# Keys of a gated recurrence: TensorE transposes replaced by VectorE block transposes and a trip through DRAM

## The chip, the core and the metric

One Trainium2 chip, one of its cores. A core has TensorE (PE in the profile; its weight loads, which overlap the matmuls, are PEld), VectorE (DVE), ScalarE (ACT), GpSimd (POOL) and SyncE (SP), each with its own instruction stream in order; they wait for each other by semaphores. SP issues nearly all DMA transfers of this kernel; sixteen DMA engines carry them out. The metric is the device time of one execution in microseconds (us); lower is better.

## The reference

An encoder block over 1024 tokens of width 1024: one large projection, dilated window attention, a bidirectional gated linear recurrence (HGRN2), a gated merge, and a feed-forward layer. Only the recurrence is touched. Per head (8 heads, keys and values of width 128) and per direction it computes, in chunks:

```python
    cum = jnp.cumsum(logf.reshape(b, h, n, c, kd), axis=3)
    q_dec = q * jnp.exp(cum)
    k_inv = k * jnp.exp(-cum)
    ...
    u = jnp.einsum('bhnck,bhncv->bhnkv', k * jnp.exp(cum_last - cum), v)
    ...
    def step(state, inp):
        d, uu = inp
        return d[..., None] * state + uu, state
```

The sum `u` over the tokens of a chunk is a matrix product, keys transposed times values. TensorE contracts over the partition dimension, so it needs the keys with tokens on the partitions. The kernel holds them the other way round, with the 128 key features on the partitions and tokens along the row, since the decays are scans along the tokens.

## The kernel before

Everything is float32; large products are made as three products of split parts (hi x hi, lo x hi, hi x lo: lines 277 to 279). Phase 1 is the projection. `stream` (line 677) runs it as a sequence of 322 steps: tiles of output columns in a seven-product scheme (a Strassen-like one, order 1, 2, 6, 5, 7, 3, 4), each step 4 x 3 = 12 products of 128x512 into a PSUM bank named pj. After a step its bank is evacuated (`leave`, line 650) by ScalarE into `wkeep` or by VectorE into a buffer `evh`, of which there are three, and then stored to DRAM by SP (lines 578, 592, 605, 620). The weight blocks a11, a21, a12 and a22 of the next tile are loaded by SP (line 256) when their single buffers come free; VectorE forms sums of them (lines 717, 718, 722), ScalarE and GpSimd split them (lines 219 and 229).

Beside the stream run side jobs on the projections that are finished: per pair of heads two recurrence jobs (`hgrn_side`, line 1294), then the attention of a head group (`att_far`, `att_near`). A side job is a generator: `yield k` means that it goes on after k more steps of the stream (a negative number also lets the next job's first loads be issued). So the code's order sets a priority; a scheduler then lines up each engine's instructions, taking later ones where an earlier one's operands are not there yet. On the chip each engine keeps the order that came out.

`hgrn_side` does for a head: load its projections; for both directions (d = 0 and 1) gate activations on ScalarE, decay scans (line 1181) and reciprocals (line 1199) on VectorE, products on GpSimd (lines 1189 and 1202) that end as the scaled keys `st["ki", d]`, the tile `t0` or `t1`, 128 features x 1024 tokens. `hgrn_keys` (line 1210) turns them: for each half of the tokens b, four PE transposes of 128x128 against the identity into a PSUM bank `sd`, and one ScalarE copy to a buffer `hkT` (line 1217). `hgrn_states` (line 1221) multiplies `hkT` with the values `hv` (line 1232; four matmuls for the first half, three for the second), and folds the chunk states with ScalarE and VectorE (lines 1234 to 1243, tiles hS and hR). Then come the scores (lines 1257 to 1261), the outputs (line 1284) and the norm.

The buffers `hkT`, `ham`, `hsq`, `hon`, `bias` and `perm` share five slots of 128x512 (`half`, line 783). The value rows already take a similar way: `rows` (line 582) transposes 32x32 blocks on VectorE (line 589) and stores them with four DMAs that place the blocks (line 592).

When the last side job is done, the attention results are loaded and split (lines 1333 to 1336) during the last steps of the stream, so that phase 2 can begin with them.

Of the kernel before, what the change touches and what calls it, by code (L numbers as in the profile page):

```python
# [10 lines left out]
F32 = mybir.dt.float32  # L11
# [11 lines left out]
HALF = 512  # L23
# [56 lines left out]
class Block:  # L80
    evac_ahead = 1000

    def __init__(self, ctx, tc, x, ln_in_g, ln_in_b, w_in, hgrn_lb, hgrn_norm_g, w_att_up, w_hgrn_up,
                 w_o, ln1_g, ln1_b, w_ffn_in, w_ffn_out, ln2_g, ln2_b, tabs, out, dbg=None):
        self.tc, self.nc, self.ctx = tc, tc.nc, ctx
        self.x = x[0]
        self.ln = {"in": (ln_in_g, ln_in_b), "1": (ln1_g[0], ln1_b[0]), "2": (ln2_g[0], ln2_b[0])}
        self.w_in, self.lbw, self.ng = w_in[0], hgrn_lb, hgrn_norm_g[0]
        self.wa, self.wr, self.wo = w_att_up[0], w_hgrn_up[0], w_o[0]
        self.wfi, self.wfo, self.tabs, self.out = w_ffn_in[0], w_ffn_out[0], tabs, out[0]  # L90
        self.dbg = dbg or {}
        nc = self.nc

        self.npj = 0
        self.issued = {}
        self.psum = ctx.enter_context(tc.tile_pool(name="psum", bufs=1, space=PSUM))
        self.cst = ctx.enter_context(tc.tile_pool(name="cst", bufs=1))
        self.tiny = ctx.enter_context(tc.tile_pool(name="tiny", bufs=1))
        self.spare = self.pad(self.cst, CST_PAD)
        self.wpool = self.pool("wp", "right")  # L100
        self.wp = self.wpool.__enter__()
        dram = ctx.enter_context(tc.tile_pool(name="dram", bufs=1, space=DRAM))

        def scratch(name, n):
            if name in self.dbg:
                return [self.dbg[name][i] for i in range(n)]
            return [dram.tile([128, 1024], F32, name=f"{name}{i}") for i in range(n)]

        self.att_d = scratch("att", 4)
        self.rec_d = scratch("rec", 8)  # L110
        self.tg_d = scratch("tg", 16)
        self.n1_d = scratch("n1", 8)
        self.ahs_d = scratch("ahs", 8)
        self.hg_d = [{n: dram.tile([128, T], F32, name=f"hg{h}{n}") for n in ("t0", "t1", "q", "g")}
                     for h in range(8)]
        self.at_d = [{(k, g): dram.tile([128, T], F32, name=f"at{j}{k}{g}") for k in "qk" for g in range(3)}
                     for j in range(4)]
        for h in range(8):
            self.hg_d[h]["v"] = dram.tile([T, 128], F32, name=f"hg{h}v")
        for j in range(4):  # L120
            self.at_d[j].update({("v", g): dram.tile([T, 128], F32, name=f"at{j}v{g}") for g in range(3)})
        self.w_d = [dram.tile([32, 128], F32, name=f"wd{j}") for j in range(4)]
        self.td = [dram.tile([128, 4, HALF], F32, name=f"td{i}") for i in range(3)]
        self.gd = {p: dram.tile([128, NF // 2, HALF], F32, name=f"gd{p}") for p in range(1, 8)}
        self.consts()
# [1081 lines left out]
        nc.vector.scalar_tensor_tensor(qd[:, :, near], q3[:, :, near], CQ, qd[:, :, near], op0=OP.mult, op1=OP.mult)  # L1207
        yield

    def hgrn_keys(self, st, d):  # L1210

        nc, out = self.nc, []
        for b in (0, 1) if d == 0 else (1, 0):
            pt, kT = self.ps_sd(), self.half3("hkT")
            for k in range(4):
                nc.tensor.transpose(pt[:, 128 * k:128 * (k + 1)], st["ki", d][:, 4 * b + k, :], self.ident)
            nc.scalar.copy(kT, pt.rearrange("p (k c) -> p k c", k=4))
            out.append(kT)
        return out

    def hgrn_states(self, st, d, kT, vT):
# [72 lines left out]
    def hgrn_side(self, h, st):  # L1294
        nc = self.nc
        vT = self.fetch_rows(5, "hv", self.hg_d[h]["v"])
        st["fa"] = self.slot(6, "fa")
        steps = [self.hgrn_dir(h, d, st) for d in range(2)]
        for _ in range(2):
            for z in steps:  # L1300
                next(z)
                yield 1
        k0 = self.hgrn_keys(st, 0)
        for z in steps:
            next(z)
        yield 2
        next(steps[0])
        yield 1
        S = {0: self.hgrn_states(st, 0, k0, vT)}
        k1 = self.hgrn_keys(st, 1)  # L1310
        yield 2
        next(steps[1])
        sg = self.fetch(8, "hg", self.hg_d[h]["g"])
        yield 1
        S[1] = self.hgrn_states(st, 1, k1, vT)
        yield 3
        am = [self.hgrn_scores(st, b) for b in range(2)]
        yield -3
        on = [self.hgrn_out(st, b, am[b], vT, S) for b in range(2)]
        yield 2  # L1320
        for b in range(2):
            pt = self.ps_sd()
            for jj in range(4):
                nc.tensor.transpose(pt[:, 128 * jj:128 * jj + 128], on[b][:, jj, :], self.ident)
            s = slice(HALF * b, HALF * (b + 1))
            nc.vector.scalar_tensor_tensor(sg[:, s], pt, self.ngc, sg[:, s], op0=OP.mult, op1=OP.mult)
        nc.scalar.dma_start(self.rec_d[h], sg)
# [733 lines left out]
```

## Time and profile before

| what | value |
|---|---|
| median of 3 runs | 2019.93 us (2014.48 to 2020.14) |
| the profiled execution's own time | 2021.5 us |
| its span, first to last instruction | 2019.7 us |
| mean granted TensorE clock | 0.997 |
| line 1216, key transposes on PE | 128, from 127.9 to 932.8 us |
| line 1217, their copies by ScalarE | 32, median 592 ns |
| line 1232, state matmuls on PE | 224, from 134.7 to 941.0 us |
| DMA, mean rate | 149 GB/s |

The page gives each engine's busy time and share of the span, then 40 slices with the busy tenths. Views by window give the same per stretch, with the number of instructions in brackets, the granted clock and the DMA engines' share. A row of a timeline has start, duration, engine, line, operation and the tiles it writes and reads. A row of the waits names who waited for whom: total, times, longest. The rows of a line's view give min/median/max; an SPq row is a DMA's issue on SP's queue. Matmuls are pipelined, so the sum of durations on PE is more than the time that they take up.

### The profile page before, as it was taken

Reading aid. Unit: us, or ns where it says so; the run is one execution under the profiler, and the core shown is the slowest. Engines: PE = TensorE matmul, PEld = TensorE weight load, DVE = VectorE, ACT = ScalarE, POOL = GpSimd, SP = SyncE. Lnnn points to the kernel's source line nnn. Section 1 sums busy time; section 2 is a strip of 40 time slices with the busy share of each in tenths; the row PEclk is TensorE's granted clock in tenths of the full one; section 3 lists DMA queues with packets and bytes.
Section 4 is the critical chain, followed back from the end, with each engine's and each line's share of the span. In section 5 each row is a group of like instructions: output and inputs, shape, how many; then the busy total and the mean of one; then the engine's idle time right before and its main releaser. Section 6 shows DMA issues by size and latency. Waiting matters only on the chain. (4 is left out here: it accounts for less than half of the span.)

```text
span 2019.7 us, 30761 instructions
## 1 busy us (share of the span) xinstructions
PE 1985.0 (98%) x10782; PEld 1644.0 (81%) x10782; DVE 1338.9 (66%) x2105; ACT 932.7 (46%) x1926; POOL 1008.1 (50%) x874
## 2 busy tenths in 40 slices
PE   7999999999999999999999999999999999999998
PEld 5688888788888888788888888887788888888886
DVE  7876645885468944778454236557776776767788
ACT  6654455554555536555464332345333333344541
POOL 5566644576446663566546562244665665620000
PEclk9999999999999999999999999999999999999999
DMA  5444545455454453445537377434434443447533
GB/s 161 138 129 140 168 113 146 127 145 170 118 149 137 135 164 104 150 136 143 152 106 210 120 254 244 149 122 145 138 131 136 138 140 129 138 166 280 167 101 124
DMA packets 369404, 301.16 MB, mean 149 GB/s; under 512 B 98721, under 2 KB 308578, under 8 KB 369250
## 3 DMA queue, kind: packets, MB, share of 16 engines
q1 hardware_dynamic: 362752, 277.94, 45.7%
q10 hardware_dynamic: 6498, 21.27, 2.8%
q8 instruction: 85, 1.39, 0.3%
q14 instruction: 69, 0.57, 0.1%
HBM read 204.96 MB, written 94.18 MB: 148 GB/s over the span
## 5 line engine op out<-in xcount | busy, mean ns | idle before, releaser
L229 POOL TENSOR_TENSOR w_lo<-wa,w_hi 128x512 fp32r<-128x512 f32 x272 | 363.4, 1345 | 268.9 <-ACT w_hi L219 255.3
L219 ACT CAST w_hi<-wa 128x512 fp32r<-128x512 f32 x272 | 168.2, 620 | 242.9 <-PE pj L278 147.3
L229 POOL TENSOR_TENSOR w_lo<-wsum,w_hi 128x512 fp32r<-128x512 f32 x88 | 127.5, 1460 | 111.9 <-PE sd L279 60.7
L229 POOL TENSOR_TENSOR w_lo<-f_raw,w_hi 128x512 fp32r<-128x512 f32 x66 | 101.1, 1540 | 51.6 <-ACT w_hi L219 50.4
L215 POOL TENSOR_TENSOR mv<-mv,mhalf 128x1 f32<-128x1 f32 x16 | 12.6, 790 | 221.7 <-DVE mv L214 221.6
L219 ACT CAST w_hi<-wsum 128x512 fp32r<-128x512 f32 x88 | 54.6, 621 | 116.7 <-PE sd L278 107.0
L277 PE MATMUL pj<-xt1hi,w_hi 128*128 128x512 f32 x252 | 100.0, 397 | 0.7 <-DVE evh L589 0.7
L219 ACT CAST gwsum<-a_raw 128x512 fp32r<-128x512 f32 (+1 forms) x78 | 48.2, 618 | 112.4 <-PE pj L278 50.1
L278 PE MATMUL pj<-xt1lo,w_hi 128*128 128x512 f32 x252 | 98.5, 391 | 0.0
L279 PE MATMUL pj<-xt1hi,w_lo 128*128 128x512 f32 x252 | 98.2, 391 | 0.0
L719 POOL TENSOR_TENSOR wa<-wa,wa 128x512 f32<-128x512 f32 x46 | 66.2, 1440 | 57.9 <-DVE wa L718 51.6
L603 DVE TENSOR_TENSOR evh<-wkeep,pj 128x512 f32<-128x512 f32 x45 | 30.8, 685 | 89.0 <-PE pj L279 52.6
L229 POOL TENSOR_TENSOR w_lo<-ws,w_hi 128x512 fp32r<-128x512 f32 x46 | 61.8, 1348 | 55.3 <-ACT w_hi L219 50.7
L747 ACT COPY wkeep<-pj 128x512 f32<-128x512 f32 x136 | 79.6, 585 | 0.2 <-DVE evh L577 0.2
L277 PE MATMUL pj<-xt2hi,w_hi 128*128 128x512 f32 x192 | 76.6, 400 | 2.0 <-ACT w_hi L219 2.0
L279 PE MATMUL pj<-xt2hi,w_lo 128*128 128x512 f32 x192 | 76.3, 397 | 2.2 <-POOL w_lo L229 2.2
L229 DVE TENSOR_TENSOR gwkeep<-a_raw,gwsum 128x512 fp32r<-128x512 f32 (+1 forms) x78 | 53.2, 682 | 37.4 <-ACT gwsum L219 34.7
L277 PE MATMUL pj<-xb11hi,w_hi 128*128 128x512 f32 x192 | 75.9, 398 | 1.5 <-DVE evh L619 1.5
L278 PE MATMUL pj<-xt2lo,w_hi 128*128 128x512 f32 x192 | 76.1, 396 | 0.7 <-DVE xt2lo L409 0.6
L277 PE MATMUL pj<-xt4hi,w_hi 128*128 128x512 f32 x192 | 75.9, 395 | 0.0
L279 PE MATMUL pj<-xb11hi,w_lo 128*128 128x512 f32 x192 | 75.4, 393 | 0.0
L278 PE MATMUL pj<-xb11lo,w_hi 128*128 128x512 f32 x192 | 75.4, 393 | 0.0
(441 smaller groups left out, 6506.0 us busy)
## 6 DMA issues: line engine op xcount, KB each, us to landing
wa<-in_w_in_dram SPq DMA_DIRECT2D x184, 256.0 KB, 3.4
f_raw<-in_w_ffn_in_dram SPq DMA_DIRECT2D x44, 512.0 KB, 4.2
a_raw<-gd SPq DMA_DIRECT2D x30, 512.0 KB, 3.7
gd<-fc SPq DMA_DIRECT2D x44, 256.0 KB, 2.0
gd<-fs SPq DMA_DIRECT2D x33, 256.0 KB, 2.1
tg<-evh SPq DMA_DIRECT2D x32, 256.0 KB, 3.3
tg<-tg SPq DMA_DIRECT2D x16, 512.0 KB, 5.6
y<-ahs SPq DMA_DIRECT2D x16, 512.0 KB, 7.8
```

The costliest lines, as they stand in the source:

```text
L215: nc.gpsimd.tensor_tensor(mv[:, 2:3], mv[:, 2:3], self.mhalf[:, 0:1], OP.pow)
L219: ins = nc.scalar.copy(hi, src) if eng_hi == "act" else nc.vector.tensor_copy(hi, src)
L229: ins = e.tensor_sub(lo, src, hi.bitcast(F32))
L277: nc.tensor.matmul(ps, whi, xhi, start=first, stop=False, **kw)
L278: nc.tensor.matmul(ps, whi, xlo, start=False, stop=False, **kw)
L279: self.product = nc.tensor.matmul(ps, wlo, xhi, start=False, stop=last, **kw).ins.name
L603: self.left(nc.vector.tensor_add(t, add, ps))
L719: nc.gpsimd.tensor_sub(a["a21"], a["a22"], a["a11"])
L747: nc.scalar.copy(t, ps)
```

## The change

The key transposes and their copies go. In their place VectorE transposes each half (128x512) in 32x32 blocks in one instruction, SP stores the result to a DRAM scratch tile `kd`, and four loads per half, one for each group of 32 partitions, bring it back into the same buffer with the blocks in their places; each piece that is moved back is 32 floats, 128 bytes. Store and loads are now two functions: both directions are turned and stored early, and the loads (`hgrn_back`) are issued later in the code. One `yield 1` becomes `yield 2`.

```diff
+        self.kd = [[dram.tile([128, HALF], F32, name=f"kd{h}{n}") for n in range(4)] for h in range(8)]
...
-    def hgrn_keys(self, st, d):
+    def hgrn_keys(self, h, st, d):
 
         nc, out = self.nc, []
         for b in (0, 1) if d == 0 else (1, 0):
-            pt, kT = self.ps_sd(), self.half3("hkT")
-            for k in range(4):
-                nc.tensor.transpose(pt[:, 128 * k:128 * (k + 1)], st["ki", d][:, 4 * b + k, :], self.ident)
-            nc.scalar.copy(kT, pt.rearrange("p (k c) -> p k c", k=4))
-            out.append(kT)
+            t, scr = self.half("hkT"), self.kd[h][2 * d + b]
+            nc.vector.transpose(t, st["ki", d][:, 4 * b:4 * b + 4, :].rearrange("p k c -> p (k c)"))
+            nc.sync.dma_start(scr, t)
+            out.append((t, scr.rearrange("(a i) (k b j) -> b i k a j", a=4, b=4, j=32)))
+        return out
+
+    def hgrn_back(self, keys):
+        out = []
+        for t, z in keys:
+            for b in range(4):
+                self.nc.sync.dma_start(t[32 * b:32 * b + 32, :].rearrange("i (k a j) -> i k a j", a=4, j=32), z[b])
+            out.append(t.rearrange("p (k c) -> p k c", k=4))
         return out
...
-        k0 = self.hgrn_keys(st, 0)
+        k0 = self.hgrn_keys(h, st, 0)
         for z in steps:
             next(z)
+        k1 = self.hgrn_keys(h, st, 1)
         yield 2
+        k0 = self.hgrn_back(k0)
         next(steps[0])
-        yield 1
+        yield 2
         S = {0: self.hgrn_states(st, 0, k0, vT)}
-        k1 = self.hgrn_keys(st, 1)
+        k1 = self.hgrn_back(k1)
         yield 2
```

What the scheduler makes of it is shown at three places of the third head (the first one behind an attention job). Rows are instructions in their engine's order; xN counts equal ones in a row. The new file's line numbers are shifted: 277 to 279 become 278 to 280, 1232 becomes 1240.

PE before, at the first state group of the third head (`t_3694` is its keys of the second direction):

```order
L277 MATMUL pj<-xt2hi,w_hi 128x512
L278 MATMUL pj<-xt2lo,w_hi 128x512
L1232 MATMUL sd<-hv,hkT 128x128 x7
L1216 MATMUL sd<-tabs_sb,t_3694 128x128 x8
L279 MATMUL pj<-xt2hi,w_lo 128x512
```

PE in the change, at the first state group of the same head:

```order
L279 MATMUL pj<-xb22lo,w_hi 128x512
L1240 MATMUL sd<-hv,hkT 128x128 x4
L280 MATMUL pj<-xb22hi,w_lo 128x512
L278 MATMUL pj<-xb22hi,w_hi 128x512
L279 MATMUL pj<-xb22lo,w_hi 128x512
L280 MATMUL pj<-xb22hi,w_lo 128x512
L278 MATMUL pj<-xt4hi,w_hi 128x512
L279 MATMUL pj<-xt4lo,w_hi 128x512
L1240 MATMUL sd<-hv,hkT 128x128 x3
```

The transposes are gone, the seven state matmuls stand in two pieces, and the first piece has moved back: it stood behind the 1232nd product of the stream (the first transposes behind the 1212th), and now stands behind the 1316th; the second direction's two pieces stand behind the 1344th and the 1353rd (before: in one piece behind the 1260th).

SP before, at the same place, begins with the load of the output gate and goes on with weight loads (`wa`), stores of evacuated banks (`at1q`, `at1v`) and loads for the next steps:

```order
L801 DMA hg<-hg2g 128x1024
L256 DMA wa_4026<-in_w_in_dram 128x4x128
L801 DMA q<-hg3q 128x1024
L256 DMA wa_4052<-in_w_in_dram 128x4x128
L256 DMA wa_4108<-in_w_in_dram 128x4x128
L256 DMA wa_4128<-in_w_in_dram 128x4x128
L578 DMA at1q_154<-evh 128x512
L256 DMA wa_4149<-in_w_in_dram 128x4x128
L592 DMA at1v_183<-evh 32x16x32 x4
```

SP in the change, from the head's first key store on:

```order
L1217 DMA kd_187<-hkT 128x512
L1217 DMA kd_188<-hkT 128x512
L257 DMA wa_4099<-in_w_in_dram 128x4x128
L1217 DMA kd_190<-hkT 128x512
L1225 DMA hkT<-kd_187 32x16x32
L1217 DMA kd_189<-hkT 128x512
L1225 DMA hkT<-kd_187 32x16x32 x3
L1225 DMA hkT<-kd_188 32x16x32
L579 DMA at1q_154<-evh 128x512
L1225 DMA hkT<-kd_188 32x16x32 x3
L1225 DMA hkT<-kd_190 32x16x32 x2
L593 DMA at1v_215<-evh 32x16x32 x4
```

Twenty transfers of the keys now stand among the stores of evacuated banks; the weight loads that stood here (the a22 blocks last) come behind the last key load.

VectorE in the change, in the same head, from the evacuation of the bank that ends with the 1212th product (line 618, before 617) to both pairs of key transposes:

```order
L618 TENSOR_TENSOR pj<-wkeep,pj 128x512
L1205 SCALAR_TENSOR_TENSOR qd<-q,fa 128x8x64
L578 TENSOR_TENSOR evh<-wkeep,pj 128x512
L723 TENSOR_TENSOR wa_3616<-wa_3616,wa_3410 128x512
L723 TENSOR_TENSOR wa_3660<-wa_3660,wa_3431 128x512
L1200 RECIPROCAL qd<-fb 128x4x64 x2
L620 SCALAR_TENSOR_TENSOR evh<-evh,pj 128x512
L1200 RECIPROCAL qd<-fb 128x4x64
L1216 STREAM_TRANSPOSE hkT<-t_3769 128x512 x2
L1205 SCALAR_TENSOR_TENSOR qd<-q,fa 128x8x64
L1216 STREAM_TRANSPOSE hkT<-t_3773 128x512 x2
```

The four transposes are inserted into VectorE's row of evacuations, weight sums and reciprocals; before, that row had none for the keys.

## The prediction

> **What bounds the kernel now.** I read the page first: its head, engine line and slices.
>
> ```profile
> span 2019.7 us, 30761 instructions
> PE 1985.0 (98%) x10782; PEld 1644.0 (81%) x10782; DVE 1338.9 (66%) x2105; ACT 932.7 (46%) x1926; POOL 1008.1 (50%) x874
> PE   7999999999999999999999999999999999999998
> ```
>
> TensorE (PE) is busy in every slice and no other engine is above 66%. An average hides stages, so I cut out the stretch in which the eight recurrence heads run, where all edits lie:
>
> ```profile
> core 0: us, PE busy (x) PEld busy (x) DVE busy (x) ACT busy (x) POOL busy (x), PEclk, DMA share, GB/s
> 100.00:200.00 100.00, 99.53 (x558) 83.77 (x557) 70.92 (x81) 49.35 (x100) 65.24 (x62) 1.00 0.46 136
> 200.00:400.00 200.00, 197.13 (x1326) 164.00 (x1326) 126.74 (x261) 105.00 (x265) 104.88 (x97) 1.00 0.49 139
> 400.00:600.00 200.00, 199.40 (x1321) 166.80 (x1317) 121.96 (x253) 100.49 (x244) 111.85 (x106) 1.00 0.52 146
> 600.00:800.00 200.00, 199.01 (x1311) 166.53 (x1310) 135.93 (x241) 104.62 (x246) 119.79 (x116) 1.00 0.48 138
> 800.00:940.00 140.00, 137.48 (x800) 115.16 (x800) 109.72 (x144) 73.26 (x165) 84.08 (x79) 0.99 0.45 129
> ```
>
> PE stands idle for only 7.5 of these 840 us, at a granted clock of 0.99 to 1.00. So PE's work here is the time: what leaves PE is won in full, and each microsecond for which PE stands before an operand is lost in full. What PE waited for between 100 and 1000 us is a short list, complete here:
>
> ```profile
> PE pj L279 <- POOL w_lo L229: 2.5, 2, 2.0
> PE pj L277 <- DVE evh L619: 1.5, 1, 1.5
> PE pj L277 <- DVE evh L589: 1.2, 1, 1.2
> PE sd L1069 <- DVE WW L1066: 1.1, 2, 0.6
> PE sd L1216 <- POOL t L1202: 1.0, 1, 1.0
> ```
>
> No transfer stands in it: as the kernel is, PE never waits for DMA here.
>
> **Part 1: the transposes leave PE.** 128 of them go: eight heads, two directions, eight each. Their busy time overlaps that of their neighbours, so I price them by start times (start, duration, then the group) in the timeline:
>
> ```profile
> 127.70 0.39 PE L277 MATMUL pj<-xt2hi,w_hi 128*128 128x512 f32 x1
> 127.93 1.03 PE L1216 MATMUL sd<-tabs_sb,t 128*128 128x128 f32 x8
> 128.72 0.48 PE L278 MATMUL pj<-xt2lo,w_hi 128*128 128x512 f32 x1
> 134.71 1.72 PE L1232 MATMUL sd<-hv,hkT 128*128 128x128 f32 x14
> 136.27 1.04 PE L1216 MATMUL sd<-tabs_sb,t 128*128 128x128 f32 x8
> 137.06 0.48 PE L277 MATMUL pj<-xt1hi,w_hi 128*128 128x512 f32 x1
> ```
>
> Eight transposes hold the stream from 127.93 to 128.72, and again from 136.27 to 137.06: 0.79 us, or 0.099 us each. 128 x 0.099 = **12.7 us off PE**. (A stream product takes 127.93 - 127.70 = 0.23 us.) The switches between product and small-matmul stretches cost a little too, but I count 25 such stretches of transposes and state matmuls before and 26 after, because the state groups now stand in pieces, so that term is nil.
>
> A rule speaks against this part's aim. The Trainium skill, "VectorE: DVE Perf Modes", section "Rules for kernel authors", says to transpose 128x128 on TensorE if a PSUM destination will do. The same page, under "The three transpose paths", gives 390 ns there (bf16); by that figure the gain would be an estimated 50 us. The start times above speak against that figure inside a dense stream, and for the rule: a PE transpose is cheap here, so there is little to win.
>
> Also gone is PE's wait for GpSimd before the transposes. Whole trace, view of line 1216:
>
> ```profile
>   POOL t L1202: 2.9, 3
> ```
>
> Three of sixteen groups met it: **2.9 us**. Together 15.6 us is the most that can be won. ScalarE loses its 32 evacuations of PSUM; it is at 46% and PE does not wait for it, so nothing is booked.
>
> **Part 2: VectorE.** 32 transposes of 128x512 are added. The same operation and shape is there already, for the value rows:
>
> ```profile
> L589 DVE STREAM_TRANSPOSE evh<-evh x30: 648/700/715, 80.1 to 958.8; 128x512 f32<-128x512 f32 x30
> ```
>
> 32 x 0.70 = 22.4 us, 2.8 us a head, on an engine that is at 61 to 78% in the windows above. On average that hides in its idle time. What is queued behind: the evacuations of the stream's banks. If VectorE is just then behind, PE pays up to these 2.8 us a head, 22 us in all; I book nothing, since the list of PE's waits holds only 2.7 us for evacuations.
>
> **Part 3: the trip through DRAM.** Each head adds 4 stores of 256 KB and 16 loads of 64 KB, all on SP's queue. The nearest rows (issue min/median/max in ns, then landing in us) are the row stores with the same 128-byte pieces in the other direction, the plain stores of 256 KB, and the 64 KB gathers from DRAM in pieces of 512 bytes:
>
> ```profile
> L592 SPq DMA_DIRECT2D hg1v<-evh x8: 319/494/507, 129.4 to 154.6; - x8
> DMA to landing us min/median/max: 1.8/2.1/6.7
> L578 SPq DMA_DIRECT2D at0k<-evh x6: 320/452/902, 148.3 to 257.3; - x6
> DMA to landing us min/median/max: 2.0/2.3/4.9
> L819 SPq DMA_DIRECT2D v<-at0v x8: 430/432/1202, 262.0 to 266.3; - x8
> DMA to landing us min/median/max: 2.9/3.8/6.6
> ```
>
> From the start of a transpose to the moment when the first state group may run: transpose 0.7, store landed 2.3, three more loads issued 3 x 0.49 = 1.5, last load landed 3.5 (between 2.9 and 3.8): **8.0 us**. A load of this very shape is not in the trace; by the row stores' 2.1 the trip is 6.6 us, by the gathers' worst 6.6 it is 11.1.
>
> Does PE arrive earlier than that? Third head, the example of the order rows. PE reached its 1212th stream product, the place of the old transposes, long before VectorE evacuated the bank finished there:
>
> ```profile
> 372.29 1.09 PE L1216 MATMUL sd<-tabs_sb,t 128*128 128x128 f32 x8
> 380.48 0.68 DVE L617 TENSOR_TENSOR pj<-wkeep,pj 128x512 f32<-128x512 f32 x1
> L1199 DVE RECIPROCAL qd<-fb x32: 1687/1740/1752, 125.5 to 941.0; 128x256 f32<-128x256 f32 x32
> ```
>
> VectorE was 8.2 us behind. In the new order three reciprocals (3 x 1.74 = 5.2) and six passes over 128x512 (6 x 0.7 = 4.2 at the pace of L589) stand from that evacuation to the key transposes: they begin about 17.6 us after product 1212, and the keys are there at 25.6. The new state group stands behind stream product 1316, which PE reaches after 104 x 0.227 = 23.6 us. PE would stand there for 2.0 us. If VectorE were not behind, nothing would be waited for. The later groups add little: from the fourth load to the sixteenth SP issues 19 transfers (12 loads and 4 row stores at 0.49, 3 plain stores at 0.45: 9.2 us), and PE has 37 products and 11 of the small matmuls, 37 x 0.227 + 11 x 0.1 = 9.5 us, of other work between.
>
> So per direction the unknown lies between 0 and 2.0 us. There are 16 directions, so **0 to 32 us** in all. I take 0.44 us each, **7 us**: half of the directions meeting the 0.9 us by which the gathers' median landing exceeds their least. It is nearer to the low end because the three waits of L1216 average 0.18 us over its sixteen groups: state groups, like those, were put where their operands come. The nearest row of a similar kind is that one, but the trip is longer and has more that can vary.
>
> **Part 4: SP and DMA time.** SP gets 16 x 0.49 + 4 x 0.45 = 9.6 us of issues per head. What is queued behind a load that waits for its store is, in the order rows, an evacuation's store, whose buffer is wanted again, and weight loads. The engines' load is read from a stretch with 128-byte row stores and one of wide transfers (columns as above):
>
> ```profile
> 130.50:131.00 0.50, 0.50 (x4) 0.42 (x3) 0.50 (x2) 0.15 (x1) 0.50 (x1) 1.00 0.81 119
> 132.50:133.00 0.50, 0.50 (x4) 0.42 (x3) 0.50 (x2) 0.50 (x2) 0.28 (x1) 1.00 0.99 336
> ```
>
> A 64 KB piece at 119 GB/s and a share of 0.81 takes about 0.45 us of all sixteen engines: 16 pieces are 7.2 us a head, against windows at a share of about 0.5. I book nothing; uncovered, it is 7.2 us x 8 = 57 us. The Trainium skill, "DMA: Bandwidth & Descriptors", Specifications, puts the least size for line rate at 512 bytes; by that rule a jam is likelier than by the average share, and the two rows above agree with its direction.
>
> **Part 5: one more step per head.** The side work ends 8 steps of 12 products later: 8 x 12 x 0.227 = 22 us. What follows it must still be ready for phase 2:
>
> ```profile
> L229 POOL TENSOR_TENSOR att_lo<-st_raw,att_hi x4: 2394/2398/2407, 1096.1 to 1106.9; 128x1024 fp32r<-128x1024 f32 x4
> L277 PE MATMUL pj<-att_hi,w_hi x64: 389/389/389, 1153.4 to 1196.2; 128*128 128x512 f32 x64
> ```
>
> The last split ends at 1106.9 + 2.4 = 1109.3 and is wanted at 1153.4: 44 us of room, 22 us after the shift. Hidden; without that cover, up to 22 us.
>
> **The sum**, against the profiled execution's own 2021.5 us: -12.7 - 2.9 + 7 = -8.6, so 2012.9. That execution lay 1.6 us above the median of 2019.93; on the scale of the median it is 2011.3, rounded to **2012**.
>
> **The rivals.**
> - *Full gain.* The state groups stand late enough everywhere and PE never waits: 2019.9 - 15.6 = 2004. For it: PE's old list has no DMA in it, and only 3 of 16 transposes waited. Against it: the sum for the third head.
> - *It cancels out*: the change does not do what it says, the freed PE time comes back as waits of 0.6 to 1.35 us per direction, 10 to 22 us: 2014 to 2026, middle 2020. For it: a trip of two landings replaces a PSUM copy.
> - *Slower: PE stands before the keys in every direction*, because VectorE's backlog starts the trip late. Place: the first state matmuls of each direction; price: 2.0 us as in the third head, 16 x 2.0 = 32; 2019.9 - 15.6 + 32 = 2036. It decides from 15.6 / 16 = 0.98 us per direction. For it: the 8.2 us of backlog in a row. Against it: a wait at the first direction leaves the second more room.
> - *Slower: the weight loads behind the keys come late.* The last weight blocks of a tile (a22) now stand behind the key loads on SP. If four of the 7.2 us of a burst reach PE in each head: 8 x 4 = 32, again 2036. For it: SP is in order. Against it: the view of the weight loads shows hardly any wait on them.
>
> ```profile
>   DVE ws L717: 4.2, 4
> ```
>
> 4.2 us in four waits in the whole run: most loads come in good time. By the 512-byte rule of the Trainium skill ("DMA: Bandwidth & Descriptors", Specifications) this would be the rival to come true.
>
> **How the numbers follow.** Chances: forecast (waits of 3 to 10 us, 2007 to 2014) 0.34; full gain 0.12; cancels 0.28; slower by late keys 0.18; slower by late weights 0.08. About 0.3%, 6 us, is what a measurement of this kernel can tell from no change. Faster is 0.34 + 0.12 = 0.46, the same 0.28, slower 0.26. The range from 2003 to 2034 takes in the full gain and most of the slower cases, and leaves out some 0.15 above and little below.
>
> **What would show it.** Right: L1216 gone from PE, its stream spaced by 0.23 us there, PE idle in 100 to 940 us grown from 7.5 to 10 to 18 us, with DMA hkT<-kd among PE's releasers. The trip: key loads landing 2.9 to 3.8 us after issue. Wrong: PE's waits for hkT above 16 us (late keys), or waits for evh, w_hi and w_lo grown by more than that (VectorE or weights), or key loads landing at 6 us and more at a DMA share near 1.

## The result and the profile after

| | before | after |
|---|---|---|
| median | 2018.59 us (2014.48 to 2020.14, 4 runs) | 2036.05 us (2035.74 to 2040.20, 4 runs) |
| ratio after / before, 95% interval | | 1.0094 [1.0074, 1.0115] |
| profiled execution, its own time | 2021.5 us | 2035.74 us |
| its span | 2019.7 us | 2033.9 us |
| mean granted TensorE clock | 0.997 | 0.993 |

The change makes the kernel slower by 0.9%; the forecast was a gain of 0.4%. The transposes did leave TensorE, and that is worth what was forecast; the trip through DRAM costs two and a half times that gain. One execution of e1 (3310.8 us) and one of e4 (2478.9 us) ran at a granted clock of 0.56 and 0.75; the medians and ratios of the experiments leave these two out.

The head of the page after, and its engine line:

```profile
span 2033.9 us, 30808 instructions
PE 1980.4 (97%) x10654; PEld 1634.6 (80%) x10654; DVE 1345.2 (66%) x2137; ACT 920.9 (45%) x1894; POOL 1008.0 (50%) x874
```

PE is busy for 4.6 us less than before (1985.0) in a span that is 14.2 us longer: the loss is not more work, it is waiting and clock. Where it arises is read from the first product of phase 2 (view of the tile `att_hi`; the first of the two start times):

```profile
L278 PE MATMUL pj<-att_hi,w_hi x64: 389/389/389, 1166.2 to 1209.1; 128*128 128x512 f32 x64
```

Before it began at 1153.4 us, now at 1166.2: 12.8 of the 14.2 us are lost ahead of it, in phase 1. The windows of the stretch with the recurrence heads, which before added up to 7.5 us of idle PE at a clock of 0.99 to 1.00:

```profile
core 0: us, PE busy (x) PEld busy (x) DVE busy (x) ACT busy (x) POOL busy (x), PEclk, DMA share, GB/s
100.00:200.00 100.00, 100.00 (x548) 84.09 (x547) 76.10 (x89) 47.13 (x95) 66.96 (x63) 1.00 0.61 164
200.00:400.00 200.00, 192.76 (x1226) 158.71 (x1225) 125.84 (x253) 95.53 (x234) 106.65 (x95) 0.99 0.54 147
400.00:600.00 200.00, 195.03 (x1287) 162.12 (x1286) 124.29 (x257) 104.70 (x262) 108.28 (x102) 0.99 0.55 150
600.00:800.00 200.00, 192.55 (x1168) 159.70 (x1167) 135.24 (x225) 96.09 (x220) 117.94 (x115) 0.98 0.60 164
800.00:940.00 140.00, 137.32 (x895) 114.17 (x894) 91.44 (x159) 70.72 (x159) 72.49 (x73) 0.98 0.54 151
```

840 - 817.7 = 22.3 us are idle now, and the clock has fallen to 0.98 in the later windows. The first window, with one head in it, has no idle time at all. PE's waits between 100 and 1000 us, complete, as before:

```profile
PE sd L1240 <- DMA hkT<-kd: 6.3, 7, 2.1
PE pj L278 <- DVE evh L578: 5.0, 2, 3.9
PE sd L1268 <- ACT hS L1242: 3.7, 3, 1.9
PE pj L278 <- DVE evh L620: 3.1, 2, 1.7
PE sd L1265 <- ACT hS L1242: 1.9, 1, 1.9
PE pj L278 <- ACT wkeep L748: 1.8, 2, 1.0
PE pj L280 <- POOL w_lo L230: 1.7, 2, 1.4
PE sd L1240 <- issue: 0.9, 1, 0.9
PE sd L1240 <- PE pj L280: 0.3, 1, 0.3
```

They sum to 24.7 us, against 7.3 before. Only a quarter of them name the keys. And behind some of them, or within them, the clock is halved. The windows below are the stretches between 100 and 1000 us for which the trace records it, the clock is the third number from the end:

```profile
381.90:385.30 3.40, 3.40 (x9) 2.67 (x9) 3.40 (x4) 0.04 (x1) 3.03 (x3) 0.50 0.74 228
416.10:419.50 3.40, 3.40 (x26) 2.90 (x23) 3.40 (x6) 1.11 (x3) 1.75 (x2) 0.50 0.72 160
668.60:675.40 6.80, 5.44 (x33) 4.56 (x34) 5.42 (x11) 4.38 (x13) 3.11 (x3) 0.50 1.02 345
880.30:887.10 6.80, 6.17 (x15) 4.81 (x16) 6.80 (x7) 0.92 (x2) 5.42 (x6) 0.50 0.35 97
```

The first lies behind a wait of 3.88 us for L578, which ends at 381.40; the second behind one of 1.92 us for hS (415.48); the third among two for hS, 1.91 and 1.65 us (667.44 and 669.96); the fourth begins in a wait of 1.71 us for L620 (880.93), behind one of 0.96 us for `wkeep` (878.52).

20.4 us at half speed lose 10.2 us at the most; in the profiled execution before there was one such stretch of 3.4 us (856.4 to 859.8), 1.7 us lost. The balance of the heads: -12.7 (transposes) + 24.7 - 7.3 (waits) + 10.2 - 1.7 (clock) = +13.2, measured 12.8. (Both executions have one more stretch at half speed ahead of the heads, 6.8 us before and 3.4 us now; with it the balance is +11.5.) So the time is accounted for to within about 1 us; what is left to explain is the waits that do not name the keys.

The third head shows where two of them come from. SP's timeline, from the first key load on:

```profile
391.74 0.62 SPq L1225 DMA_DIRECT2D hkT<-kd  x1
...
396.45 3.31 SPq L1225 DMA_DIRECT2D hkT<-kd  x5
399.86 2.20 SPq L593 DMA_DIRECT2D at1v<-evh  x4
402.10 2.60 SPq L1225 DMA_DIRECT2D hkT<-kd  x4
...
406.73 0.56 SPq L1225 DMA_DIRECT2D hkT<-kd  x1
407.39 0.61 SPq L257 DMA_DIRECT2D wa<-in_w_in_dram  x1
```

SP issues almost without a pause for 15.6 us (391.74 to 407.39), and the weight block `wa` comes last. ScalarE, meanwhile, and then PE:

```profile
411.19 0.62 ACT L220 CAST w_hi<-wa 128x512 fp32r<-128x512 f32 x1 [5.43 <-DMA wa<-in_w_in_dram]
411.72 1.14 ACT L1242 ACTIVATE hS<-sd,dec 128x128 f32<-128x128 f32 x4
...
414.56 0.87 ACT L1242 ACTIVATE hS<-sd,dec 128x128 f32<-128x128 f32 x3
```

```profile
415.48 0.27 PE L1268 MATMUL sd<-qd,t 128*64 128x64 f32 x1 [1.92 <-ACT hS L1242]
```

ScalarE stands for 5.43 us before the cast of a block whose load was issued too late: at 407.39, and 3.8 us later the cast begins. The states' copies (L1242), which need nothing of that block, stand behind the cast; PE waits 1.92 us for the bank that they empty; at 416.1 the clock is halved. This is a chain, SP to ScalarE to PE, that the list of PE's waits shows only by its last link. At 665.7 us it is there again, with 4.53 us. The transfers themselves are hardly slower. The weight loads between 100 and 1000 us, from issue to landing:

```profile
L257 SPq DMA_DIRECT2D wa<-in_w_in_dram x144: 367/384/1163, 102.1 to 998.1; - x144
DMA to landing us min/median/max: 2.8/3.6/8.9
```

Before the change the median was 3.4 us, and in e2 below, which has no trip, 3.5 us with a worst case of 8.5. In the burst (391.7 to 407.4) the DMA engines' share is 0.71, so they are not full there; from 661 to 665.7, at the second place, it is 0.89.

### The profile page after: what moved, and what is told of

Same layout as the page of the kernel before. It is cut to its first block, busy times and chain, and to the rows that moved or that the text cites. A ratio compares the mean times of both kernels' runs of the same rounds, so it can differ in the third digit from the quotient of the medians.

```text
span 2033.9 us, 30808 instructions
## 1 busy us (share of the span) xinstructions
PE 1980.4 (97%) x10654; PEld 1634.6 (80%) x10654; DVE 1345.2 (66%) x2137; ACT 920.9 (45%) x1894; POOL 1008.0 (50%) x874
## 5 line engine op out<-in xcount | busy, mean ns | idle before, releaser
L279 PE MATMUL pj<-xt4lo,w_hi 128*128 128x512 f32 x192 | 75.9, 395 | 0.0
```

The source lines that it names most:

```text
L279: nc.tensor.matmul(ps, whi, xlo, start=False, stop=False, **kw)
```

## The experiments

Two theories stand against each other. **Late keys**: what costs is that PE stands before the loads of the keys. **The queue**: what costs is that twenty transfers a head on SP put off what stands behind them. Beside them VectorE's transposes and the extra step could be the cause. Each experiment was timed in three rounds beside the kernel before; "us" is the median. e2, e5, e11, e12 and e15 do not compute the reference's result: their state products read other numbers.

| kernel | us | ratio to before, 95% interval |
|---|---|---|
| e2: no trip | 2004.11 | 0.9935 [0.9920, 0.9950] |
| e11: stores only | 2009.51 | 0.9963 [0.9947, 0.9979] |
| e15: stores, tiny loads, late states | 2011.66 | 0.9974 [0.9957, 0.9990] |
| e5: trip, unread | 2019.36 | 1.0004 [0.9993, 1.0014] |
| e12: trip unread, late states | 2029.02 | 1.0059 [1.0042, 1.0077] |
| **the change** | 2036.05 | 1.0094 [1.0074, 1.0115] |
| e16: weight loads ahead of keys | 2037.41 | 1.0100 [1.0084, 1.0115] |
| e9: stores place the blocks | 2041.36 | 1.0124 [1.0102, 1.0146] |
| e6: without the extra step | 2043.46 | 1.0128 [1.0110, 1.0147] |
| e1: key loads on ScalarE's queue | 2045.34 | 1.0138 [1.0119, 1.0156] |
| e7: half the trip | 2029.70 | 1.0056 [1.0039, 1.0073] |
| e4: before, with the extra step | 2023.63 | 1.0028 [1.0014, 1.0041] |
| e3: before, with 32 VectorE transposes | 2021.96 | 1.0016 [1.0006, 1.0026] |

### The parts that are not the trip: e3, e4, e2

e3 is the kernel before with the transposes added:

```diff
+            nc.vector.transpose(self.half("hkD"), st["ki", d][:, 4 * b:4 * b + 4, :].rearrange("p k c -> p (k c)"))
```

> The kernel before, keys turned by TensorE as ever, plus the 32 VectorE transposes of 128x512 into a buffer that nobody reads. VectorE theory: 8 to 22 us over before, 2027 to 2041, with PE's waits for DVE evh up from 2.7 us. Queue and step theory: within 4 us of before.

It is 0.16% slower, some 3 us. VectorE's 22 us of work are hidden but for that.

e4 is the kernel before with `yield 2` for `yield 1` ahead of the states of direction 0:

> The kernel before with the one yield 1 turned into yield 2, so each recurrence job takes one more step of the stream; nothing else. Step theory: 2025 to 2036, PE waits of 10 us and more for DVE evh. Queue and VectorE theory: 2014 to 2023, same as before.

It is 0.28% slower, some 6 us. In its profiled execution the longest of PE's waits is

```profile
PE pj L277 <- DVE evh L577: 4.3, 2, 3.8
```

The changed kernel has the same wait (L578 above, 3.9 us at the longest), before its third head's key loads. There is no trip in e4, so the step is enough for it. It is not the step alone that sets its length: e2, e5 and e11 below have the step too, but their state products earlier, and show 1.9 us there.

e2 is the changed kernel without stores and loads:

```diff
-            nc.sync.dma_start(scr, t)
...
-            for b in range(4):
-                self.nc.sync.dma_start(t[32 * b:32 * b + 32, :].rearrange("i (k a j) -> i k a j", a=4, j=32), z[b])
...
-                nc.tensor.matmul(ps[:, jj, :], kT[b][:, c % 4, :], vT[:, c, :], start=True, stop=True)
+                nc.tensor.matmul(ps[:, jj, :], vT[:, c, :], vT[:, c, :], start=True, stop=True)
```

> Store and loads are left out, and the state matmuls take the values in place of the keys (the recurrence's result is not the reference's), the VectorE transposes stay. Queue theory, or PE waiting for the keys: 2001 to 2010, the saving of 12.7 to 15.6 us in full, no clock drop in 200 to 940 us. VectorE theory: still 2020 to 2036, with PE waiting for DVE evh. Step theory: 2014 to 2030.

It has the full gain, 0.65%, 13 us. PE's waits between 100 and 1000 us are few (the two largest; the others add 1.8 us):

```profile
PE pj L278 <- DVE evh L620: 3.5, 3, 1.6
PE pj L278 <- DVE evh L578: 2.9, 2, 1.9
...
```

VectorE's transposes and the extra step are both in it. They are not the cause; the trip costs all of the 32 us between this and the change (1.0094 - 0.9935 = 1.6%). (With no load to wait for, e2's state products also stand earlier; e15 shows that this alone is worth little.)

### Moving the loads to another queue: e1

```diff
-                self.nc.sync.dma_start(t[32 * b:32 * b + 32, :].rearrange("i (k a j) -> i k a j", a=4, j=32), z[b])
+                self.nc.scalar.dma_start(t[32 * b:32 * b + 32, :].rearrange("i (k a j) -> i k a j", a=4, j=32), z[b])
```

> The 128 key loads are issued from ScalarE's queue; stores and all else stay. Queue theory (key loads on SP hold back weight loads and evacuation stores): ScalarE's waits for wa loads, 5.4 and 4.5 us at 411 and 666 us in the change, go; but ScalarE now spends 128 x 0.6 = 77 us on issues, so 2012 to 2028. VectorE theory (the 32 transposes come when VectorE is behind) or step theory (the extra step of the stream puts the side job at a worse place): no change from the changed kernel, 2032 to 2040.

Slower still, outside what either theory gave. ScalarE's casts stand behind the loads in its own row. From its waits, and from PE's:

```profile
ACT w_hi L220 <- DMA hkT<-kd: 11.1, 4, 5.9
```

```profile
PE sd L1240 <- DMA hkT<-kd: 15.1, 12, 2.2
PE sd L1268 <- ACT hS L1242: 5.1, 3, 2.7
```

The view of `wa` in the changed kernel shows 17.3 us, in 10 waits, in which an engine stood for a weight load; here the ten largest rows of that view, down to 3.7 us, have none for it. So the weights were late because of their place behind the key loads, with the same transfers under way. But the casts wait all the same, now behind the key loads on their own engine: the jam has moved, not gone.

### Splitting the trip: e5, e11

e5 keeps the whole trip, and only the states read the values in place of the keys:

> The changed kernel with its whole trip (VectorE transposes, stores, 128 loads), but the state products take value rows in place of the keys, so that TensorE never waits for a key load; the states are other numbers. Without the trip such a kernel took 2004, with it 2036: 32 us lie between. Theory 1 (keys reach TensorE too late: 7.2 us of waits for hkT, and the half clock that follows them): the trip is harmless when nobody waits for it, 2004 to 2010. Theory 2 (the trip fills SP's queue, so weight loads and stores behind it are late): only the 7 us of waits for hkT and 2 to 3 us of half clock go, 2022 to 2030; ScalarE's waits for wa stay near 10 us in the heads.

2019.4 lies between the two: 14 us above e2 with nobody waiting for a key, 17 us below the change. Late keys as the only cause falls (2004 to 2010 was its forecast), and the queue as put (2022 to 2030) is too high. PE's longest waits are now for VectorE:

```profile
PE sd L1334 <- DVE hon L1299: 6.4, 3, 2.9
```

The longest of them ends at 679.07 us, and it has a late weight block behind it too: VectorE stands 5.22 us for `wa` until 668.29, the sums of the blocks and GpSimd's work on them come late, GpSimd's `hss` stands behind that work, VectorE waits 5.71 us for `hss`, and PE 2.92 us for `hon`.

e11 leaves out the loads of e5 as well and keeps the stores:

> The kernel with the unread trip (2019.4) without its 128 loads: VectorE's transposes and the 32 stores stay, the state products take value rows, so the states are other numbers. Without stores and loads it was 2004.1: 15 us lie between. Theory 1 (the burst of 16 loads a head holds back what stands behind it on SP): 2004 to 2008. Theory 2 (the four stores, which stand on SP and wait there for VectorE's transposes, hold it back: SP stood some 29 us before them in the heads): 2012 to 2018, and ScalarE and VectorE wait for wa as long as with the loads.

2009.5, between the two forecasts: the 32 stores cost 0.28%, about 6 us, the unread loads another 0.41%, about 8 us; the intervals of these two steps are about 4 us wide to either side. The waits for `wa` are those without loads: 6.7 us (4.2 in e2, 21.2 in e5). So it is the loads that make the weights late. How the stores cost their 6 us stays open: PE's waits hardly differ (8.7 us, 8.2 in e2), but the profiled execution of e11 has 10.2 us at half speed ahead of phase 2, that of e2 none.

### Where the rest comes from: e12, e15

In e5 the scheduler, which has no load to wait for, also puts the state products earlier: in the third head behind stream product 1188 to 1248, in the change 1316 to 1353. e12 puts them back by an order alone, without a wait:

```diff
-                nc.tensor.matmul(ps[:, jj, :], vT[:, c, :], vT[:, c, :], start=True, stop=True)
+                self.behind(nc.tensor.matmul(ps[:, jj, :], vT[:, c, :], vT[:, c, :], start=True, stop=True), kT[b])
```

Here `kT[b]` is the name of the half's last load, and `behind` sets an order without a semaphore.

> The unread trip (2019.4) again, but the state products stand as late in TensorE's order as in the changed kernel (within 8 stream products of it, in the third head 1308 against 1316, where the unread trip had 1188 to 1248); they still take value rows, so they wait for no load. The changed kernel is 2036: 17 us lie between. Theory 1 (the waits for keys themselves, 7.2 us, and the half clock behind them): 2018 to 2022, no wait for the states grown. Theory 2 (the states come some 100 products later in each head, so ScalarE's hS and what follows are pressed together): 2026 to 2034, with TensorE's waits for hS at 4 us and more.

2029.0, ten above e5, seven below the change. From PE's waits, and ScalarE's timeline at the longest of them:

```profile
PE sd L1268 <- ACT hS L1242: 11.0, 3, 4.7
```

```profile
659.15 0.62 ACT L220 CAST w_hi<-wa 128x512 fp32r<-128x512 f32 x1 [5.93 <-DMA wa<-in_w_in_dram]
...
659.98 0.35 ACT L1242 ACTIVATE hS<-sd,dec 128x128 f32<-128x128 f32 x1
```

It is the same chain as in the third head above, with no key waited for: states that come late fall behind the cast that waits for the late weights. In e5 weight loads are waited for as long (the view of `wa` has 21.2 us there, in 11 waits; 17.3 in 10 in the change), but the states are through by then, and PE meets the lateness only through `hon`.

e15 asks whether late states cost by themselves. The 16 loads of a head become 4 of one row, with everything else as in e12:

```diff
-            out.append((t, scr.rearrange("(a i) (k b j) -> b i k a j", a=4, b=4, j=32)))
+            out.append((t, scr))
...
-            for b in range(4):
-                ld = self.nc.sync.dma_start(t[32 * b:32 * b + 32, :].rearrange("i (k a j) -> i k a j", a=4, j=32), z[b])
+            ld = self.nc.sync.dma_start(t[0:1, :], z[0:1, :])
```

> The late unread trip (2029) with its 16 loads of 64 KB a head replaced by 4 of one row (2 KB), so SP has 12 issues a head less and moves almost nothing back; the state products, still on value rows, stand nearly as late (third head 1297, then 1308, and 1188 to 1248 where they are early). With stores alone and early states it was 2009.5. Theory 1 (late states cost by themselves): 2009.5 + 9.6 = 2019 and more, waits for hS near 11 us again. Theory 2 (they cost because the weight loads stand behind the key loads, so a cast of ScalarE that waits for a late block holds the states' copies): 2009 to 2013, waits for hS below 2 us.

2011.7: they do not, as far as an interval of some 0.2% can tell. The waits for hS are gone; the list of PE's waits begins with

```profile
PE pj L278 <- DVE evh L578: 5.0, 2, 3.9
PE pj L280 <- POOL w_lo L230: 2.9, 4, 1.9
...
```

Late states cost together with late weights, hardly alone, and the weights are late with the sixteen loads (the view of `wa` has 5.3 us of waits for them here). The 3.9 us at L578 stay, as in e4. (Its states stand a little earlier than in e12, 1297 against 1308 in the third head.)

### Changing the order on SP: e16, e9, e6, e7

e16 is the whole change; only the loads that go through one helper, the weight blocks above all, get a higher priority, so that they are issued between the key loads:

```diff
-        self.ordered("loads", self.nc.sync.dma_start(dst, src))
+        with self.tc.high_priority(offset=self.evac_ahead):
+            self.ordered("loads", self.nc.sync.dma_start(dst, src))
```

> The changed kernel, all of it, with only the order on SP changed: a weight block's load is issued before the key loads that wait beside it (in the third head the load of the block that came late stands after 1 of 16 key loads' place instead of after all 16). Each key load moves back by up to three weight loads, about 1.2 us; the state products stand some 3 to 10 products later. Theory 1 (weight loads behind the key loads): waits for hS (5.6 us) and ScalarE's for wa (10 us) go, waits for hkT stay at 7 to 10 us: 2022 to 2029. Theory 2 (late keys): waits for hkT grow by 16 x up to 1 us: 2036 to 2045.

No change in the time, and yet both forecasts came true in part. The two lists against the change's: ScalarE waits 2.7 us for `wa` instead of 10.0, PE 0.5 us for hS instead of 5.6, and 11.2 us instead of 6.3 for the keys:

```profile
PE sd L1241 <- DMA hkT<-kd: 11.2, 11, 2.5
PE pj L279 <- DVE evh L579: 6.2, 3, 3.8
PE sd L1241 <- DMA wa<-in_w_in_dram: 2.2, 1, 2.2
PE sd L1269 <- ACT hS L1243: 0.5, 1, 0.5
```

```profile
ACT w_hi L220 <- DMA wa<-in_w_in_dram: 2.7, 1, 2.7
```

In this order, as in the change's, whoever stands behind on SP pays: the order decided who, and hardly how much (PE's waits sum to 27.5 us, 24.7 in the change). So "late keys" and "the queue" look like two ends of one cause.

e9 lets the stores place the blocks: sixteen stores and four plain loads a head.

```diff
-            nc.sync.dma_start(scr, t)
-            out.append((t, scr.rearrange("(a i) (k b j) -> b i k a j", a=4, b=4, j=32)))
+            z = scr.rearrange("(b i) (k a j) -> a i k b j", b=4, a=4, j=32)
+            for a in range(4):
+                nc.sync.dma_start(z[a], t[32 * a:32 * a + 32, :].rearrange("i (k b j) -> i k b j", b=4, j=32))
+            out.append((t, scr))
...
-            for b in range(4):
-                self.nc.sync.dma_start(t[32 * b:32 * b + 32, :].rearrange("i (k a j) -> i k a j", a=4, j=32), z[b])
+            self.nc.sync.dma_start(t, z)
```

> The blocks are placed by the store, not by the load: 16 stores of 64 KB in 128-byte pieces and 4 plain loads of 256 KB a head, in place of 4 plain stores and 16 loads. Bytes, pieces and the number of transfers stay. Theory 1 (late keys): one load instead of four stands behind each landing, so the keys come 3 x 0.63 = 1.9 us sooner per half; of 7.2 us of waits about 5 go, with some half clock: 2026 to 2032. Theory 2 (weight loads behind a burst of 16 loads): the burst behind the landing shrinks from 10 us to 1.5 us, but 16 stores of about 0.45 us stand on SP earlier: 2012 to 2026. Theory 3 (the small pieces load the DMA engines, wherever they are): no change, 2036.

2041, above all three forecasts: twenty issues a head are no cheaper for placing the blocks with the store. PE stands 13.6 us before keys (6.3 in the change), ScalarE 13.4 us before `wa` (10.0). Issues, bytes and small pieces are as many as in the change, so e9 does not part these.

e6 is the change with `yield 1` ahead of the states, as before the change:

> The changed kernel without its extra step: the state products of direction 0 stand one step after the key loads instead of two. In the kernel before, the extra step cost 4 to 6 us (one wait of 3.8 us for VectorE at 381 us and the half clock behind it). If costs add up: 2030 to 2033, with that wait gone. If the keys are late, the shorter way makes their waits longer than 7.2 us: 2036 to 2045.

2043. Waits of 2.4 and 1.6 us, for L590 and L578, stand in the place of that of 3.9, but the states stand closer behind their keys: waits for hS are 8.7 us (5.6 in the change), for keys 8.1 us. Costs don't add: with the trip, the extra step gains more than it costs.

e7 has direction 0's keys by TensorE and ScalarE, as before, and direction 1's by the trip:

> Direction 0's keys by TensorE's transposes and ScalarE's copies as before the change, direction 1's by VectorE and the trip; the extra step stays. TensorE keeps 64 transposes, 6.3 us. If the cost of the trip goes with its number of transfers, half of 32 us stays: 2004 + 6 + 16 = 2026. If what costs is the long burst of both directions on SP, half a burst is hidden by the buffers that the weight loads have in hand: 2010 to 2018. If late keys in the first direction are the cost, 2004 + 6 + less than 8: 2010 to 2018 too, but then with waits for hkT near 3 us, and ScalarE's waits for wa still near 10 us.

2029.7, nearest to the linear 2026: less e2's 2004 and 6 us of transposes, half the transfers cost 19 of 32 us. So the buffers that are in hand do not hide half a burst.

No kernel that does the whole computation was faster than the one before. e2's 2004 is what the freed TensorE is worth; a faster kernel would need a trip that costs less than 15 us, and none of the four ways tried here (other queue, other order, blocks placed on the store, half) came near.

## Why the prediction was wrong

**Right.** Part 1's sum, 15.6 us off PE at the most: e2 gains 0.65% [0.50, 0.80], 10 to 16 us, with VectorE's transposes and the extra step in it. Its 2.9 us of waits for GpSimd were read too high: 1.9 us of them are waits of PE's weight loads, and the list of PE's own waits has 1.0. Part 2, VectorE nil: 3 us by e3. Part 3, 7 us of PE waiting for keys: the change's view of `hkT` has 6.3 us on the matmuls and 0.9 us on their weight loads, and the last rung, e12 to the change, is worth 0.35%, 7 us. The size is right; the example was not. In the third head, where 2.0 us was summed, the first state group began at 398.53 us without a wait for keys: PE had already stood 3.88 us before VectorE at 381.4, a wait that the sum did not have. The landing was forecast at 2.9 to 3.8 us:

```profile
L1225 SPq DMA_DIRECT2D hkT<-kd x128: 562/634/1285, 131.8 to 982.0; - x128
...
DMA to landing us min/median/max: 2.3/2.9/5.5
```

**The step that failed is Part 4**: "I book nothing; uncovered, it is 7.2 us x 8 = 57 us". It was priced as load on the DMA engines, against an average share. The runs show the queue in its place: e16 and e1, with the same bytes under way, change who waits and gain nothing, and e15, with twelve issues a head and their bytes taken away, has no such waits. (Bytes and issues went together in e15, so it does not part them; e1, e16 and the weight loads' landing, 3.6 us against 3.5 without the trip, speak for the place in the queue.) The 16 issues were put at 0.49 us each after the row stores; they take 0.634, and with what stands among them the burst above is 15.6 us long. By the ratios, taken as differences of the ladder: stores 0.28%, loads 0.41%, the states caught behind late weights 0.55%; 6 + 8 + 11 = 25 us where nothing was booked. (The stores' 6 us are a cost of the trip whose way to PE is open, and in the last of the three the wait at L578 grew by 2.1 us as well.)

**The rival that came true** is the last one, late weight loads, put at 0.08 and 2036. It was marked down because 4.2 us was all that VectorE's weight sums had waited. That view shows how often the old queue was late, not how much room it had. That its price, 2036, is the measured time to the microsecond is luck: it was to come from "four of the 7.2 us" a head, and the 32 us came from stores, loads, caught states and 7 us of late keys together. Nor was the road the one described: the cast of a late block holds ScalarE, and the block's own users hardly appear among PE's waits (w_lo 1.7 us). What was missing was the question which other work stands behind the waiting cast: Part 4 named the queue behind the loads on SP, but not the one behind the cast on ScalarE.

By the 512-byte rule of the Trainium skill ("DMA: Bandwidth & Descriptors", Specifications), which the prediction put beside this rival, it would come true through a jam of small pieces. The trace does not show that: the key loads land in 2.9 us, in the range of the forecast, and the weight loads in 3.6.

**Part 5**, the extra step hidden by 44 us of room: the room was there, but e4 loses some 6 us elsewhere. The step shifts the stream against VectorE's scans and reciprocals, and a wait of 3.8 us arises at 381 us. The right question was not only what follows the last job, but what now stands beside what.

**Not in the sum at all**: the clock. The prediction said "each microsecond for which PE stands before an operand is lost in full". It can be more than that: in the profiled execution 17.4 us of added waits brought up to 8.5 us of lost clock. The rate is not fixed: e16's execution has 27.5 us of waits and 10.2 us at half speed among the heads, e1's 36.5 and 13.6, the change's 24.7 and 20.4.

**The signs** that were named served in part: PE's waits for hkT stayed below 16 us, so late keys alone were out; PE idle grew from 7.5 to 22.3 us, past the 10 to 18. The sign for late weights stayed silent: PE's waits for evh grew only from 2.7 to 8.1 us and those for w_lo fell from 2.5 to 1.7, since the lateness reached PE through hS (5.6 us, none before).

## What to carry to other kernels

An in-order queue with slack is not free: before adding transfers to it, find for each of those behind them when its data is wanted, and follow the wait one engine further, to the unrelated work behind the instruction that will wait. When a wait is removed, and another of the same size takes its place, suspect the length of the queue: here another order (e16) and another queue (e1) gained nothing, and the kernels with fewer transfers (e7, e15) were faster. And where TensorE is the bound, look at its clock behind waits of about 2 us: in the change the added waits cost up to one and a half times their length.

## What was not expected of the hardware

The clock can be halved behind waits of about 2 us. In the changed kernel the wait of 1.92 us that ends at 415.5 is followed by half speed from 416.1 to 419.5, and in the kernel before one of 2.03 us:

```profile
855.47 0.50 PE L279 MATMUL pj<-xb22hi,w_lo 128*128 128x512 f32 x1 [2.03 <-POOL w_lo L229]
```

```profile
856.40:859.80 3.40, 3.40 (x10) 2.63 (x9) 3.40 (x5) 0.62 (x1) 3.40 (x6) 0.50 0.39 113
```

The stretches last 3.41 or 6.83 us, and in the changed kernel their starts (381.9, 416.1, 668.6, 880.3) lie 10, 74 and 62 times 3.413 us apart, to the resolution of these numbers. Not every such wait brings one: that of 2.1 us for keys (the longest of L1240's, ending at 972.7) did not. The Trainium skill, "TensorE: Matmul & The Clock Gate", "Why this matters for your kernels", says to leave no gap of more than about 3 us. These two rows show the loss behind gaps of 1.9 and 2.0 us, so for this kernel the measurement, and not the page's 3 us, decides. Its "What's actually happening" describes windows of 3413 ns that run freely. The lengths and the spacing of the stretches agree with that; that it is also the reason why a gap of 2 us only sometimes counts is an inference, no run here varied it.
